# Residual gate early, four accumulator banks in the last jobs, another order of the last operands, and a shorter chain in the final norm

## The chip, the core and the metric

The kernel runs on one core of one Trainium2 chip. The time is the device time of one execution in microseconds (us). TensorE (PE in the profile) does the matrix products, VectorE (DVE), ScalarE (ACT) and GpSimd (POOL) the elementwise work, and SyncE (SP) issues nearly all transfers; a few go out on ACT's queue. Each engine and each queue takes its instructions strictly in the order in which the program gives them, and an instruction that waits for a semaphore holds up all behind it on that engine.

## The reference, cut to what matters

All is float32: a sequence of 2048 positions and a model width of 1024.

```python
mod = silu(c) @ w_mod + b_mod                       # (1, 3 * 1024)
shift, scale, gate = split(mod, 3)
h = rms_norm(x, g_norm) * (1 + scale) + shift
x_rnn, z_rnn, q, k, v, z_attn, g_r, g_a = split(h @ w_in, 8)      # each (2048, 1024)
y_rnn = (rg_lru(conv(x_rnn)) * silu(z_rnn)) @ w_out_rnn
y_attn = (dilated_attention(q, k, v) * silu(z_attn)) @ w_out_attn
merged = sigmoid(g_r + b_r) * y_rnn + sigmoid(g_a + b_a) * y_attn
x = x + gate * (merged @ w_o)
out = x * rsqrt(mean(x * x, -1) + 1e-6) * g_final
```

## The kernel before, in words

Every float32 product is three matmuls. Each operand is split into `hi`, its rounding to the short type fp32r, and `lo`, the rest; `mm3` (line 150) adds hi*hi, hi*lo and lo*hi. Line 158 (`hi_act`) is the rounding on ACT, line 164 (`lo_pool`) the subtraction on POOL, line 167 (`lo_dve`) the same on DVE. A split is therefore an ACT instruction followed by one on POOL or DVE, each on 128x512 numbers. The large products (`h @ w_in` and `merged @ w_o`) use a scheme of seven products of half-size blocks with sums of blocks as operands, in the manner of Strassen.

The order of all instructions is written by hand. Work beside the products is hung into them at a numbered place: a *slot* of the values, a *step* of the last jobs, a number of products done in the projections and the output. What is hung at a place is emitted ahead of the matmuls of that place, on whatever engine and queue it belongs to.

The stages that matter here, in order:

- **The second values** (about 727 to 828 us of the profiled execution): 8 runs of 4 slots; a slot is 24 matmuls with 256 columns. DVE, ACT and POOL at the same time build `hx` (the normed input), sums of its blocks in `t` and their splits into `T`, the operands of the next projections (lines 575 to 590, 738, 158, 167). `residual_gate` computes `gate` in these slots: `load` (line 1267) fetches a 128x512 piece `gw` of w_mod, `add` (lines 1272, 1274) multiplies it with a column of silu(c) into an accumulator, `total` sums the accumulator over its partitions by one matmul with ones, `bias` (line 1281) adds b_mod and sends the row to `gateD`, from which line 1962 later reads it back, spread over 128 partitions (`gate_b`).
- **The second projections** begin with product X, whose operand is `T`, and whose weights are raw pieces `R` (line 253) split into `S`.
- **The last jobs** (1981.95 to 2082.05 us): jobs 6 and 7 of the products with w_out_rnn and w_out_attn, 16 tiles t = 48 to 63 of 128x512, alternately of one and of the other job after the first four. A tile takes 8 steps of one `mm3` each; its accumulator is one PSUM bank. Its `load_g` (line 1851) fetches the two arrays `fg` with which the tile is merged, `evict` (lines 1856, 1858) multiplies and adds them on DVE, and `store` (line 1863) writes the sum to `meT`. There are four `fg` buffers, two tiles' worth, so the load for tile t waits for the store of tile t-2. The operands `yh`, `yl` of job 7 live in four of the 14 tiles `F`; they come from `oT` (line 359) and are split in place. Beside all that run the w_o operands: raw pieces `or` in four buffers (lines 1968, 1971), number i from 0 to 27, four to each of the seven operands in the order B11, T2, T3, T1, B21, T4, B22; those of B pieces are multiplied with `gate_b` (line 1976) and all are split into `F`.
- **The output products** (from 2082.05 us): 8 rounds x of seven products with 12 matmuls each: X (B11), Z (T2), W (T3), V (T1), X again (B21), Y (T4), and V again (B22), which is put behind the first product of the next round. V is a bank of pool `pf` in even rounds and of `pj` in odd ones. Their left operands are sums of blocks of `meT` (raw `R`, sums `s`, splits `S`). Lines 2170 and 2175 add banks into `u`, line 2124 adds banks to the rows `xo` (V twice, after T1 and after B22, and the second product may start only behind the first reading), line 2157 adds `u` on POOL.
- **The final norm** of each of the 16 row tiles: ACT squares and sums two halves (line 2135; the last two row tiles, line 2098), DVE adds the halves (line 2138, or 2106), line 171 scales and adds eps, ACT takes the root, and `rstd_last` (lines 176 to 180) forms the reciprocal with one Newton step; line 2145 scales the row, line 2147 stores it. These small instructions have 128x1 numbers, and four of a tile's seven on DVE have two tensor operands.

## Time and profile before

| | us |
|---|---|
| median of 3 runs (lowest, highest) | 2271.62 (2269.47, 2272.5) |
| the profiled execution, its time | 2262.82 |
| its span | 2261.0 |
| PE busy | 2202.5 |
| DVE busy | 1494.9 |
| ACT busy | 1293.2 |
| POOL busy | 1199.7 |

The profile is of one execution, which was 8.8 us shorter than the median. Durations, starts and waits in what follows are all of that execution. In a row of the timeline the first number is the start in us, the second how long the group lasted from its first start to its last end, `x12` is the number of instructions put together, and the bracket tells how long the engine was idle before it and what ended that. `L1274` is line 1274 of the kernel. SPq is SP's queue of transfers.

### The profile page before, as it was taken

The numbers are of one execution on the slowest core, as the hardware profiler recorded it, in microseconds if no ns is written. First come the engines' busy times: TensorE is split into PE (matmuls) and PEld (weight loads), VectorE is DVE, ScalarE is ACT, GpSimd is POOL, SyncE is SP. The second block draws the span as 40 slices with busy tenths as digits, with TensorE's granted clock in tenths as the row PEclk, the third lists the DMA queues.
The fourth block names the chain that finished last, engine by engine and source line by source line (L and its number), as shares of the span: only waits on it lengthen the run. The fifth ranks groups of instructions, "written<-read, shape, count | busy, mean of one in ns | idle before, by whom it ended". The sixth has DMA issues, their size and how long they took to land. (4 is left out here: it accounts for less than half of the span.)

```text
span 2261.0 us, 34371 instructions
## 1 busy us (share of the span) xinstructions
PE 2202.5 (97%) x11358; PEld 1846.4 (82%) x11359; DVE 1494.9 (66%) x2487; ACT 1293.2 (57%) x2560; POOL 1199.7 (53%) x898
## 2 busy tenths in 40 slices
PE   9999999999999999999999999999999999989898
PEld 5998888888877988888888887889889898867776
DVE  5578788778566665555545364466677878654898
ACT  3547667678543436656667511567678878532333
POOL 2267677676567345445444312356565666333666
PEclk9999999999999999999999999999999999999999
DMA  8354665565897556786887889989988787788543
GB/s 282 89 170 172 197 216 179 192 225 186 249 284 228 166 183 219 241 257 223 246 252 242 266 304 303 298 268 281 283 274 269 230 267 241 244 279 254 163 149 131
DMA packets 455434, 520.20 MB, mean 230 GB/s; under 512 B 90360, under 2 KB 333268, under 8 KB 454232
## 3 DMA queue, kind: packets, MB, share of 16 engines
q1 hardware_dynamic: 427492, 434.95, 63.3%
q10 hardware_dynamic: 27572, 83.00, 9.7%
q8 instruction: 90, 1.47, 0.3%
q14 instruction: 88, 0.72, 0.1%
q0 software_dynamic: 192, 0.05, 0.0%
HBM read 340.67 MB, written 177.21 MB: 229 GB/s over the span
## 5 line engine op out<-in xcount | busy, mean ns | idle before, releaser
L164 POOL TENSOR_TENSOR S<-R,S 128x512 fp32r<-128x512 f32 x278 | 407.9, 1473 | 401.5 <-ACT S L158 355.0
L150 PE MATMUL X<-T,S 128*128 128x512 f32 x1344 | 333.7, 397 | 6.1 <-ACT S L158 3.8
L150 PE MATMUL V<-T,S 128*128 128x512 f32 x1344 | 331.2, 395 | 0.0
L150 PEld LDWEIGHTS X<-T,S 128*128 128x128 f32 x1344 | 254.1, 190 | 67.6 <-ACT S L158 4.5
L150 PE MATMUL pj<-yh,S 128*128 128x512 f32 x896 | 302.2, 395 | 5.1 <-DMA S<-wD 3.3
L150 PEld LDWEIGHTS V<-T,S 128*128 128x128 f32 x1344 | 252.3, 188 | 58.3
L158 ACT ACTIVATE S<-R 128x512 fp32r<-128x512 f32 x278 | 170.8, 622 | 137.7 <-DMA R<-in_w_in_dram 114.8
L164 POOL TENSOR_TENSOR S<-s,S 128x512 fp32r<-128x512 f32 x108 | 160.4, 1485 | 144.3 <-ACT S L158 114.2
L150 PEld LDWEIGHTS pj<-yh,S 128*128 128x128 f32 x896 | 169.1, 189 | 41.0 <-DVE fg L1858 2.9
L150 PE MATMUL pj<-yl,S 128*128 128x512 f32 x448 | 176.4, 394 | 2.3 <-DVE yl L167 1.4
L1543 ACT ACTIVATE pp<-pp,st 128x256 f32<-128x256 f32 (+3 forms) x256 | 133.3, 522 | 74.7 <-DVE st L1542 74.3
L150 PE MATMUL Z<-T,S 128*128 128x512 f32 x672 | 165.5, 395 | 0.0
L150 PE MATMUL Y<-T,S 128*128 128x512 f32 x672 | 165.5, 395 | 0.0
L150 PE MATMUL W<-T,S 128*128 128x512 f32 x672 | 165.4, 395 | 0.0
L150 PEld LDWEIGHTS Z<-T,S 128*128 128x128 f32 x672 | 126.5, 188 | 30.5 <-issue 0.9
L150 PEld LDWEIGHTS Y<-T,S 128*128 128x128 f32 x672 | 126.5, 188 | 29.3
L150 PEld LDWEIGHTS W<-T,S 128*128 128x128 f32 x672 | 126.4, 188 | 29.3
L167 DVE TENSOR_TENSOR ptl<-pT,pth 128x384 fp32r<-128x384 f32 (+1 forms) x160 | 97.7, 627 | 48.8 <-ACT pth L158 46.6
L960 DVE SCALAR_TENSOR_TENSOR xc<-xr,par,xc 128x512 f32<-128x512 f32 x96 | 97.0, 1011 | 49.7 <-ACT xc L954 47.4
L1542 DVE CUSTOM_DVE_ANT_0 pp<-sc,msk 128x256 f32<-128x256 f32 (+3 forms) x256 | 104.1, 448 | 37.2 <-PE sc L150 35.0
L158 ACT ACTIVATE S<-s 128x512 fp32r<-128x512 f32 x108 | 67.3, 623 | 102.3 <-DVE s L290 44.7
L164 POOL TENSOR_TENSOR kq<-kraw,kq 128x512 fp32r<-128x512 f32 (+1 forms) x64 | 101.2, 1592 | 42.0 <-ACT kq L158 32.4
(367 smaller groups left out, 4840.6 us busy)
## 6 DMA issues: line engine op xcount, KB each, us to landing
sD<-S ACTq DMA_DIRECT2D x118, 512.0 KB, 3.8
S<-sD SPq DMA_DIRECT2D x118, 512.0 KB, 4.6
S<-wD SPq DMA_DIRECT2D x100, 512.0 KB, 5.4
R<-in_w_in_dram SPq DMA_DIRECT2D x196, 256.0 KB, 4.4
wD<-s ACTq DMA_DIRECT2D x64, 256.0 KB, 3.8
T<-in_w_mod_dram SPq DMA_DIRECT2D x8, 1024.0 KB, 12.1
vN<-ev SPq DMA_DIRECT2D x64, 128.0 KB, 2.8
zaT<-ev SPq DMA_DIRECT2D x32, 256.0 KB, 3.2
```

The costliest lines, as they stand in the source:

```text
L150: nc.tensor.matmul(o, lhsT=l, rhs=r, start=st, stop=sp, **kw)
L158: nc.scalar.activation(o, i, AF.Copy)
L164: nc.gpsimd.tensor_tensor(o, i, h.bitcast(F32), ALU.subtract)
L167: nc.vector.tensor_tensor(o, i, h.bitcast(F32), ALU.subtract)
L960: nc.vector.scalar_tensor_tensor(xc, xr[:, i : i + CH], cw(i), xc, ALU.mult, ALU.add)
L1542: nc.vector.tensor_tensor_reduce(pdst, s_ps, mask, 1.0, 3e38, ALU.add, ALU.min, m_)
L1543: nc.scalar.activation(pdst, pdst, AF.Exp, bias=m_, scale=-1.0, accum_out=l_)
```

## The change

Four parts, which touch different stages.

1. `residual_gate`: the 16 pieces are loaded at slots 0 to 15 and not 2 to 25, and each is added two slots later. There are three buffers `gw` instead of two, and each half of the gate has its own accumulator (`s1`, `s2`). `total` of half 0 stands at slot 10 and of half 1 at slot 19 (before: slot 16, and in the first products of the next projections), `bias` two slots later. The row of b_mod takes a `gw` buffer.
2. The last jobs: every third and fourth tile accumulates in the banks Z and W of the output products, so that four banks take turns; `evict` is hung at step 3 of the next tile (before: 1), `store` at step 6 (before: 5). The operands of job 7 are all loaded within job 6 and split there at other steps. Of the last two tiles, that of job 7 comes first.
3. The last operands of w_o: T4 (pieces 20 to 23) is split at steps 121 to 125 of 128, beside the last tile, and no longer in the output products; B22 (pieces 24 to 27) is loaded at steps 124 to 126 and at the start of the output products, and gated and split piece by piece, alternately on POOL and DVE.
4. The final norm: the squares are scaled so that their sum is the mean; the sum of halves and eps is one tensor-scalar instruction whose scalar is a column; the two multiplications of the Newton step are one such instruction, and the last multiplication is another. So five small DVE instructions stand where there were seven, none with two tensor operands.

Nothing else moves on any engine.

The end of the second values on DVE, before (`hx`, `t` and `T` are parts of the projections' operands, `s` the gate's accumulator, `ca` silu(c)):

```order
L1274 SCALAR_TENSOR_TENSOR s_1199_6837<-gw_7685,ca_194,s_1199_6837 128x512
L575 TENSOR_TENSOR t_1324_7831<-hx_7162,hx_7158 128x512
L577 TENSOR_TENSOR hx_7158<-hx_7158,T_6617 128x512
L167 TENSOR_TENSOR T_7484<-t_1321_7795,T_7483 128x512
L579 TENSOR_TENSOR hx_7158<-hx_7158,T_6618 128x512
L1274 SCALAR_TENSOR_TENSOR s_1199_6837<-gw_7717,ca_194,s_1199_6837 128x512
L584 TENSOR_TENSOR hx_7162<-hx_7162,hx_7158 128x512
L587 TENSOR_TENSOR t_1328_7898<-T_6768,hx_7162 128x512
L167 TENSOR_TENSOR T_7478<-hx_7158,T_7477 128x512
L167 TENSOR_TENSOR T_7480<-hx_7162,T_7479 128x512
L590 TENSOR_TENSOR t_1328_7898<-t_1328_7898,T_6769 128x512
L167 TENSOR_TENSOR T_7484<-t_1328_7898,T_7483 128x512
```

and with the change:

```order
L575 TENSOR_TENSOR t_1328_7842<-hx_7173,hx_7169 128x512
L577 TENSOR_TENSOR hx_7169<-hx_7169,T_6617 128x512
L167 TENSOR_TENSOR T_7509<-t_1326_7809,T_7508 128x512
L579 TENSOR_TENSOR hx_7169<-hx_7169,T_6618 128x512
L584 TENSOR_TENSOR hx_7173<-hx_7173,hx_7169 128x512
L587 TENSOR_TENSOR t_1331_7906<-T_6768,hx_7173 128x512
L167 TENSOR_TENSOR T_7503<-hx_7169,T_7502 128x512
L167 TENSOR_TENSOR T_7505<-hx_7173,T_7504 128x512
L590 TENSOR_TENSOR t_1331_7906<-t_1331_7906,T_6769 128x512
L167 TENSOR_TENSOR T_7509<-t_1331_7906,T_7508 128x512
```

The four additions of line 1274 that stood in this stretch (two here shown, two right behind it) are gone from it.

The start of job 6 on SP's queue, before (`fg` the arrays of a tile's merge, `S` split weights, `R` raw operands of job 7, `meT` the merged result):

```order
L359 DMA R_3926_20687<-oT 128x512
L359 DMA R_3927_20692<-oT 128x512
L1863 DMA meT<-fg_20597 128x512
L359 DMA R_3938_20725<-oT 128x512
L353 DMA S_3939_20727<-wD 128x1024
L359 DMA R_3942_20738<-oT 128x512
L359 DMA R_3943_20745<-oT 128x512
L1962 DMA gate_b_20716<-gateD 128x1024
L1851 DMA fg_20750<-gaT 128x512
L1851 DMA fg_20752<-mrT 128x512
L359 DMA R_3946_20757<-oT 128x512
L1863 DMA meT<-fg_20668 128x512
```

and with the change:

```order
L353 DMA S_3927_20684<-wD 128x1024
L1864 DMA meT<-fg_20599 128x512
L359 DMA R_3938_20723<-oT 128x512
L353 DMA S_3939_20725<-wD 128x1024
L359 DMA R_3942_20734<-oT 128x512
L359 DMA R_3943_20739<-oT 128x512
L1962 DMA gate_b_20714<-gateD 128x1024
L1852 DMA fg_20744<-gaT 128x512
L1852 DMA fg_20746<-mrT 128x512
L359 DMA R_3946_20751<-oT 128x512
L359 DMA R_3947_20761<-oT 128x512
L1864 DMA meT<-fg_20670 128x512
```

The two loads `R` that stood ahead of the first store are gone from there (the load `S` ahead of them in the first list with the change stands just above the rows of before); between the two `fg` of the next tile and the second store there are two loads `R` and not one.

The first round of the output products on DVE, before (`or` the raw pieces 24 to 27, `F` their splits, `u` sums of banks; the sum `u<-Z` of line 2170 stands two rows above the first):

```order
L2032 TENSOR_TENSOR s_4084_21553<-s_4083_21552,R_4057_21421 128x512
L1976 TENSOR_TENSOR or_21507<-or_21507,gate_b_20716 128x512
L1976 TENSOR_TENSOR or_21509<-or_21509,gate_b_20716 128x512
L1976 TENSOR_TENSOR or_21511<-or_21511,gate_b_20716 128x512
L1976 TENSOR_TENSOR or_21513<-or_21513,gate_b_20716 128x512
L2175 TENSOR_TENSOR u_4086_21563<-W_21539,u_4081_21536 128x512
L2041 TENSOR_TENSOR R_4062_21445<-R_4057_21421,R_4062_21445 128x512
L167 TENSOR_TENSOR F_21587<-or_21507,F_21586 128x512
L167 TENSOR_TENSOR F_21587<-or_21509,F_21586 128x512
L167 TENSOR_TENSOR F_21587<-or_21511,F_21586 128x512
L167 TENSOR_TENSOR F_21587<-or_21513,F_21586 128x512
L2124 TENSOR_TENSOR xo_21478<-V_21567,xo_21478 128x512
```

and with the change:

```order
L1976 TENSOR_TENSOR or_21451<-or_21451,gate_b_20714 128x512
L1976 TENSOR_TENSOR or_21463<-or_21463,gate_b_20714 128x512
L1976 TENSOR_TENSOR or_21469<-or_21469,gate_b_20714 128x512
L1976 TENSOR_TENSOR or_21498<-or_21498,gate_b_20714 128x512
L2182 TENSOR_TENSOR u_4085_21546<-Z_21521,u_4079_21519 128x512
L2036 TENSOR_TENSOR s_4087_21562<-R_4067_21458,R_4072_21489 128x512
L2037 TENSOR_TENSOR s_4088_21563<-s_4087_21562,R_4059_21423 128x512
L167 TENSOR_TENSOR F_21540<-or_21463,F_21539 128x512
L2187 TENSOR_TENSOR u_4090_21573<-W_21549,u_4085_21546 128x512
L2046 TENSOR_TENSOR R_4067_21458<-R_4059_21423,R_4067_21458 128x512
L167 TENSOR_TENSOR F_21540<-or_21498,F_21539 128x512
L2140 TENSOR_TENSOR xo_21496<-V_21577,xo_21496 128x512
```

The four multiplications by `gate_b` now stand ahead of the sum `u<-Z` (line 2182 with the change), two of the four subtractions of line 167 have gone to POOL, the other two are spread out ahead of line 2124 (2140 with the change).

SP's queue at the same place, before:

```order
L2020 DMA R_4062_21445<-meT 128x4x128
L1863 DMA meT<-fg_21390 128x512
L1863 DMA meT<-fg_21435 128x512
L2020 DMA R_4065_21471<-meT 128x4x128
L2037 DMA xo_21476<-in_x_dram 128x1024
L2037 DMA xo_21478<-in_x_dram 128x1024
L1971 DMA or_21507<-in_w_o_dram 128x512
L1971 DMA or_21509<-in_w_o_dram 128x512
L1971 DMA or_21511<-in_w_o_dram 128x512
L1971 DMA or_21513<-in_w_o_dram 128x512
```

and with the change:

```order
L1971 DMA or_21451<-in_w_o_dram 128x512
L2025 DMA R_4067_21458<-meT 128x4x128
L1971 DMA or_21463<-in_w_o_dram 128x512
L1971 DMA or_21469<-in_w_o_dram 128x512
L1864 DMA meT<-fg_21392 128x512
L1864 DMA meT<-fg_21444 128x512
L2025 DMA R_4072_21489<-meT 128x4x128
L2042 DMA xo_21494<-in_x_dram 128x1024
L2042 DMA xo_21496<-in_x_dram 128x1024
L1971 DMA or_21498<-in_w_o_dram 128x512
```

Three of the four loads of `or` have moved ahead of the last two stores; the fourth is still behind them, and behind a load `R` and two loads `xo`.

The diff, cut to its core:

```diff
     def residual_gate(ep, plan):
-        acc, row = (T(wq, [P, KH, P], F32, name, bufs=1)[:].rearrange("p k m -> p (k m)") for name in ("s1", "s2"))
-        row = row[:1]
-        w = {}
+        acc = [T(wq, [P, KH, P], F32, name, bufs=1)[:].rearrange("p k m -> p (k m)") for name in ("s1", "s2")]
+        w, row = {}, {}
...
+        def piece():
+            return T(ep, [P, CH], F32, "gw", bufs=3)
...
-            w[q, k] = T(ep, [P, CH], F32, "gw", bufs=2)
+            w[q, k] = piece()
...
         def total(q):
+            row[q] = piece()
+            nc.sync.dma_start(row[q][:1, :], b_mod[0:1, 2 * D + q * CH : 2 * D + (q + 1) * CH])
             w["pt"] = T(pg, [P, CH], F32, "pg")
-            mm(w["pt"][:1, :], ones[:, 0:1], acc, True, True)
+            mm(w["pt"][:1, :], ones[:, 0:1], acc[q], True, True)
...
         for q in range(2):
             for k in range(KT):
-                i = 2 + 13 * q + (3 * k) // 2
+                i = KT * q + k
                 at_slot(i, lambda q=q, k=k: load(q, k))
-                at_slot(i + 3, lambda q=q, k=k: add(q, k))
-            at_slot(5 + 13 * q, lambda q=q: nc.sync.dma_start(row, b_mod[0:1, 2 * D + q * CH : 2 * D + (q + 1) * CH]))
-            if not q:
-                at_slot(16, lambda: total(0))
-                at_slot(17, lambda: bias(0))
-        later(1, lambda: total(1))
-        later(2, lambda: bias(1))
+                at_slot(i + 2, lambda q=q, k=k: add(q, k))
+            at_slot(10 + 9 * q, lambda q=q: total(q))
+            at_slot(12 + 9 * q, lambda q=q: bias(q))
...
-        tiles += [(LAST_HEAD + i, m) for m in range(2, KT) for i in range(2)]
+        tiles += [(LAST_HEAD + (i ^ (m == KT - 1)), m) for m in range(2, KT) for i in range(2)]
...
-            ps = T(pj, [P, CH], F32, "pj")
+            ps = T(pj, [P, CH], F32, "pj") if j < LAST_HEAD or t % 4 < 2 else FP["bank"](t % 4 - 2)
...
-                if k == 1 and t:
+                if k == (1 if j < LAST_HEAD else 3) and t:
                     evict(t - 1, last)
                 if k == 3:
                     load_g(t)
-                if k == (7 if j < LAST_HEAD else 5) and t:
+                if k == (7 if j < LAST_HEAD else 6) and t:
                     store(t - 1)
...
-                            if k in (5, 6):
-                                load_y(j + 2, k - 5)
...
-                    if i in (0, 1, 2, 3, 6, 7):
-                        load_y(j + 1, i + 2 if i < 4 else i)
-                    if i in (1, 2, 5, 6, 8, 9, 11, 12):
-                        split_y(LAST_HEAD + 1, (1, 2, 5, 6, 8, 9, 11, 12).index(i))
+                    if i in (0, 1, 2, 3, 5, 6, 7, 8):
+                        load_y(LAST_HEAD + 1, i - (i > 3))
+                    if i in (4, 5, 6, 7, 10, 11, 12, 13):
+                        split_y(LAST_HEAD + 1, i - (4 if i < 8 else 6))
...
+        FP["bank"] = lambda i: T(pf, [P, CH], F32, "ZW"[i])
...
-            (lo_dve if i % 2 or i >= 20 else lo_pool)(F[name][1][:, k, :], raw_o.pop(i)[:], F[name][0][:, k, :])
+            (lo_dve if i % 2 else lo_pool)(F[name][1][:, k, :], raw_o.pop(i)[:], F[name][0][:, k, :])
...
-            if i < 20:
+            if i >= 20:
+                at_step(101 + i, lambda i=i: hi_o(i))
+                at_step(102 + i, lambda i=i: lo_o(i))
+                if i > 20:
+                    at_step(103 + i, lambda i=i: load_o(i + 3))
+            else:
...
-        late_parts = [(0, hi_o, i) for i in range(20, 24)] + [(0, lo_o, i) for i in range(20, 24)]
-        late_parts += [(1, load_o, i) for i in range(24, 28)] + [(3, gate_o, i) for i in range(24, 28)]
-        late_parts += [(4, fn, i) for fn in (hi_o, lo_o) for i in range(24, 28)]
+        late_parts = [(0, load_o, 27)]
+        for i in range(24, 28):
+            late_parts += [(d + (i - 24) // 2, fn, i) for d, fn in ((1, gate_o), (2, hi_o), (3, lo_o))]
...
+        def first_root(ss):
+            nc.vector.tensor_scalar(ss[:, 0], ss[:, 0], ss[:, 3], EPS, ALU.add, ALU.add)
+            nc.scalar.activation(ss[:, 1], ss[:, 0], AF.Sqrt)
+
+        def last_root(ss):
+            v, y, t = (ss[:, i] for i in range(3))
+            nc.vector.reciprocal(y, y)
+            nc.vector.tensor_scalar(t, y, y, v, ALU.mult, ALU.mult)
+            nc.vector.tensor_scalar(t, t, -0.5, 1.5, ALU.mult, ALU.add)
+            nc.vector.tensor_scalar(y, y, t, None, ALU.mult)
...
-            nc.scalar.activation(jk[:], xo[:, cols], AF.Square, accum_out=ss[:, 3 if whole else 0])
+            nc.scalar.activation(jk[:], xo[:, cols], AF.Square, scale=D ** -0.5, accum_out=ss[:, 3 if whole else 0])
...
-                tt(ss[:, 0], ss[:, 0], ss[:, 3], ALU.add)
-                rstd(ss)
+                first_root(ss)
+                last_root(ss)
```

20 lines of the change are left out of this document (9 added, 11 removed).

## The prediction

> **What bounds the kernel now.** PE is busy for 2202.5 of 2261.0 us, so only the stretches where it is not can be won; I looked for them with a list of 20-us windows, then read the waits of PE there, and the timeline at each. These are the windows that matter (length; busy us of PE, weight loads, DVE, ACT, POOL; granted clock, share of DMA, GB/s):
>
> ```profile
> 800.00:820.00 20.00, 18.24 (x151) 17.84 (x149) 19.14 (x20) 8.93 (x16) 10.36 (x8) 1.00 0.35 101
> 820.00:840.00 20.00, 16.29 (x76) 12.90 (x77) 6.17 (x8) 5.06 (x9) 5.44 (x4) 0.83 0.71 224
> 1980.00:2000.00 20.00, 14.91 (x59) 11.41 (x57) 7.53 (x9) 5.12 (x9) 6.84 (x6) 0.91 0.88 273
> 2100.00:2120.00 20.00, 12.87 (x45) 9.94 (x45) 17.18 (x23) 8.76 (x19) 13.65 (x10) 0.74 0.34 107
> 2120.00:2140.00 20.00, 20.00 (x88) 16.35 (x87) 19.44 (x28) 7.37 (x18) 14.09 (x12) 1.00 0.52 157
> ```
>
> PE loses 1.8 and 3.7 us at the end of the values (with DVE at 19.14 of 20 ahead of it), 5.1 at the start of job 6 and 7.1 in the first output round, the clock falling below 1 in the last three of these windows; in the output rounds PE is full but DVE is too (19.44 of 20). What PE waited for from 1940 us to the end (total, times, longest):
>
> ```profile
> PE V L150 <- DVE xo L2124: 8.8, 3, 7.1
> PE pj L150 <- DVE fg L1856: 5.6, 6, 2.6
> PE pj L150 <- DMA S<-wD: 2.5, 1, 2.5
> PE pj L150 <- DVE xo L2124: 1.7, 2, 1.2
> ```
>
> That is 18.6 us, and slow-clock time on top; at the end of the values there is one more wait, of 3.39 (below). Every part of the change touches one of these waits, and nothing else in the order moves, so I cost them one by one.
>
> **Term 1, the gate in the values.** The chain that ends the stage:
>
> ```profile
> 822.71 0.68 DVE L590 TENSOR_TENSOR t<-t,T 128x512 f32<-128x512 f32 x1
> 823.42 0.63 ACT L158 ACTIVATE T<-t 128x512 fp32r<-128x512 f32 x1 [3.78 <-DVE t L590]
> 826.62 0.44 SPq L253 DMA_DIRECT2D R<-in_w_in_dram  x1
> 830.06 0.63 ACT L158 ACTIVATE S<-R 128x512 fp32r<-128x512 f32 x1 [5.04 <-DMA R<-in_w_in_dram]
> 830.75 1.03 PE L150 MATMUL X<-T,S 128*128 128x512 f32 x2 [3.39 <-ACT S L158]
> L1272 DVE TENSOR_SCALAR s<-gw,ca x2: 477/478/479, 744.4 to 788.8; 128x512 f32<-128x512 f32 x2
> L1274 DVE SCALAR_TENSOR_TENSOR s<-gw,ca,s x14: 739/746/1771, 748.8 to 825.5; 128x512 f32<-128x512 f32 x14
> ```
>
> Late DVE holds ACT's split of `t`; ACT's copies of the values come behind it, their stores hold SP's queue, and the weights `R` that X needs stand in that queue behind them. So X starts as late as DVE is. DVE works without a gap from about 776 us to the end of L590. In that stretch stand seven additions, the first multiplication of half 1 and one `bias`; with the change, which adds the last piece at slot 17 and puts `total` and `bias` of half 1 at slots 19 and 21, there are four additions and one `bias`. Three additions at the median 0.746 and one multiplication at 0.478 go: X comes 2.7 us earlier. Against it: the gate crowds into the first slots, where `total` of half 0 needs the eighth addition; I reckon 0.2 us of waiting there. Part of X runs at half clock, and I leave that as it is. SP's queue will stand before the `gw` loads up to some 6 us, waiting for a buffer; the raw weights behind these are used eight slots after their load, and a slot is 24 matmuls, so that covers it. The gain is bounded by the wait of 3.39 and, if X's clock stays full, one X of twelve matmuls (2.94 in a later row), 6.3 in all; the loss, if the crowd delays the first `hx`, by one addition in its slow form, 1.77. **-2.5**.
>
> **Term 2, the last jobs.**
>
> ```profile
> 1988.00 4.93 SPq L359 DMA_DIRECT2D R<-oT  x2
> 1990.03 0.47 PE L150 MATMUL pj<-yh,S 128*128 128x512 f32 x1 [2.48 <-DMA S<-wD]
> 1993.45 0.42 SPq L1851 DMA_DIRECT2D fg<-gaT  x1
> 1999.96 6.08 PE L150 MATMUL pj<-F,S 128*128 128x512 f32 x24 [2.61 <-DVE fg L1856]
> 2081.51 0.56 SPq L1851 DMA_DIRECT2D fg<-gaT  x1
> 2084.84 2.95 PE L150 MATMUL Z<-F,S 128*128 128x512 f32 x12
> 2086.34 0.69 DVE L1856 TENSOR_TENSOR fg<-pj,fg 128x512 f32<-128x512 f32 x1 [3.17 <-DMA fg<-gaT]
> 2087.63 2.94 PE L150 MATMUL W<-F,S 128*128 128x512 f32 x12
> ...
> SPq L1851 <- DMA meT<-fg: 27.7, 10, 3.8
> ...
> meT<-fg SPq DMA_DIRECT2D x16, 256.0 KB, 5.0
> R<-oT SPq DMA_DIRECT2D x6, 256.0 KB, 6.9
> ```
>
> The loads of `fg` set the pace, not the banks: from the load at 1993.45 (tile 48) to that at 2081.51 (tile 63) are 15 tiles in 88.06 us, 5.87 each, where 24 matmuls need 5.58 (from Z's start to W's, 12 of them in 2.79). Each load waits for the store two tiles back to land (27.7 us of SP's waits). Four banks don't shorten that loop; they only let PE run ahead of it by two tiles more. But PE pays at the end: product W takes the bank of tile 63 and waits for its `evict`. So the gain is how much sooner tile 63 is merged. The loop starts sooner, since the load for tile 48 stood behind two `R` of job 7 for which SP waited (4.93 with their issue, row at 1988.00); with the change two loads `R` fewer stand ahead of that `fg` pair. Of the 4.93 about 1 is issue and another 1 goes to the store that now stands ahead; I take 2.9 us, so `evict` of tile 63 ends at 2085.7 and not at 2088.6, and W, now freed by its first instruction, can start at about 2083.4, 4.2 us before 2087.63. From the PE side the excess of tiles 48 to 63 over 5.58 us each is 11.4 us, so PE could be there in time.
>
> The cost is in job 7's operands: its pieces 4 to 7 are loaded behind the splits of pieces 0 to 3 and needed four steps into tile 50 (1999.96 less its wait of 2.61, and half of 5.58 on: 2000.1). The first leave about when the row at 1988.00 does, some 0.6 later; ready is 1988.6 plus two landings L, so PE waits S = 2L - 11.5: none at the 5.0 us of a store, 2.3 at the 6.9 of `R<-oT`. I take none, for these loads leave before the merge traffic fills the queue, and keep 2.3 for the range. **-4.2 at W**, of which the next term says what reaches the end.
>
> **Term 3, the first output round.**
>
> ```profile
> 2090.68 2.32 SPq L1971 DMA_DIRECT2D or<-in_w_o_dram  x4
> 2097.09 3.02 DVE L1976 TENSOR_TENSOR or<-or,gate_b 128x512 f32<-128x512 f32 x4 [2.05 <-DMA or<-in_w_o_dram]
> 2098.66 2.96 PE L150 MATMUL X<-F,S 128*128 128x512 f32 x12
> 2101.23 6.76 DVE L167 TENSOR_TENSOR F<-or,F 128x512 fp32r<-128x512 f32 x4
> 2108.74 5.46 PE L150 MATMUL V<-F,S 128*128 128x512 f32 x12 [7.13 <-DVE xo L2124]
> 2114.00 1.27 PE L150 MATMUL Z<-F,S 128*128 128x512 f32 x4
> ```
>
> B22's raw pieces are issued at 2090.68, land 6.4 us later, are gated, and then four subtractions take 6.76 us on DVE (1.7 each: POOL is at work on tensors of its own), and the addition that frees V stands behind them. V costs 7.13 of waiting, and 5.26 us to the next product where 2.79 is the rule, 2.5 of half clock: 9.6 in all. With the change pieces 24 to 26 come earlier, beside the last tile, but piece 27 stands behind two stores, a load `R` and two `xo` on SP. The second store waits for `evict` of tile 63 (2085.7), so it leaves at about 2088.1 and lands at 2094.5. Its gating stands on DVE **ahead** of `u<-Z`, which then comes at about 2095 and not at 2091.60, and on POOL the addition of `u` to `xo` stands ahead of the split that product X of round 1 needs. So X of round 1 starts at about 2098.3, as before, though PE is there at 2094.5 (the next wait: about 3.8 us). POOL has two of the four subtractions; the second comes behind two `xo` and one `S`, 2104 to 2106 by POOL's row-to-row pace of 1.3 to 1.7. V then runs till some 2107.5 with part of it at half clock. Z of round 1 starts at 2107.5 and not at 2114.0: **-6.5 for terms 2 and 3 together**. Bounds: all 9.6 of term 3 and 4.2 of term 2 gone is -13.8; only the slack between the two orders of the four subtractions, 2 of 1.7 us less on DVE, is -2.
>
> **Term 4, the norm's small instructions.**
>
> ```profile
> L177 DVE TENSOR_TENSOR ss<-ss x16: 159/814/1283, 2115.0 to 2255.6; 128x1 f32<-128x1 f32 x16
> L178 DVE TENSOR_TENSOR ss<-ss x16: 159/1210/1226, 2116.4 to 2255.8; 128x1 f32<-128x1 f32 x16
> L179 DVE TENSOR_SCALAR ss<-ss x16: 153/154/156, 2116.5 to 2256.0; 128x1 f32<-128x1 f32 x16
> L2138 DVE TENSOR_TENSOR ss<-ss x14: 144/1165/1246, 2111.7 to 2241.5; 128x1 f32<-128x1 f32 x14
> ...
> 2235.14 2.95 PE L150 MATMUL Z<-F,S 128*128 128x512 f32 x12
> ```
>
> On one number per partition the form with two tensors takes up to 1.28 us, the tensor-scalar form never over 0.156: the first waits for POOL and the second does not. The three slow ones, 3.19 us a row tile by their medians, become two pointer forms. No row shows a pointer form of 128x1; between 0.154 (its nearest kin) and 1.21 I take 0.2, since both shapes and forms are those of L179 but for where the scalar lies. That frees 2.8 us of DVE in each 10 us, and the waits of the rounds go: from Z of round 1 (2114.00) to Z of round 7 (2235.14) are 121.1 us, where six rounds of seven products at 2.79 need 117.2. Excess 3.9; PE's waits for line 2124 but for the one of 7.1 sum to 3.4. **-3.3** (0 to -3.9).
>
> The Trainium skill says the opposite may happen: in SBUF — State Buffer, section "Who interferes with whom", `tensor_scalar` may enter a mode with both ports that shuts GpSimd out or waits for it. By that rule the merged ones would wait as L178 does, and this term would be near 0. L179 in the rows above, with 154 in the middle of 16, does not bear that out.
>
> **Term 5, the tail.**
>
> ```profile
> 2248.95 2.88 PE L150 MATMUL pj<-F,S 128*128 128x512 f32 x12
> 2253.09 0.68 DVE L2092 TENSOR_TENSOR xo<-pj,xo 128x512 f32<-128x512 f32 x1
> ```
>
> PE ends at 2251.83 (2248.95 and 2.88); the last addition waits until the first row tile's chain is through, 2253.09. That chain loses two instructions and its slow forms, some 0.8 us by the slow forms in the rows of term 4, and the last row tile's own loses two instructions at 0.15: **-1.1** (-0.2 to -1.5).
>
> **Sum.** -2.5 - 6.5 - 3.3 - 1.1 = -13.4. The profiled execution took 2262.82, so 2249.4 on its scale. It was 8.8 us under the median of 2271.62, to which the change is measured: **2258**.
>
> **The rivals.**
> - *Piece 27 does not hold anything.* If it lands in time, or the queue is shorter, all 13.8 of terms 2 and 3 come through: -20.7, 2251. For it: the medians of landings above are 5.0 and 6.9 us, and the stores ahead could leave at once. Against: the order itself, with gating ahead of `u<-Z`.
> - *The merged norm instructions wait like the old ones.* Then term 4 falls away and term 5 shrinks to 0.2: -9.2, 2262. For it, beside the page named above: no pointer form of this size is in the trace.
> - *Job 7's operands come late.* At a landing of 6.9, S is 2.3 and the half clock that followed a gap of 2.48 (granted clock 0.91 in that window) adds 1.9, part of which is taken up by waits behind it: -10.5, 2261. The same mechanism gives the other sign: the pieces 4 to 7 wait in one queue with eight loads and the merge traffic, and if a landing takes 14.8 us, S is 18.1 and eats the 13.4 and 4.5 more: 2276 or above. The longest median in the stage is 6.9, so this needs twice the traffic's delay.
> - *The waits only move.* DVE or POOL takes back in the rounds what PE wins at V: within 4.5 us of the median, 2271. For it: DVE is at 19.4 of 20 until term 4 frees it, and POOL gets four tensors more.
>
> The Trainium skill has a rule on the half clock, in TensorE: Matmul & The Clock Gate, Part 1: after an idle window of about 3.4 us the clock falls to half. The 2.48 us before 1990.03 were followed by slow matmuls, so a shorter gap does it in this trace; by the page's rule a gap of 3.8 before X of round 1 would be sure to cost, by the row it may, and my sum has it in V's end.
>
> **How the numbers follow.** Chances: the forecast 0.43, all of term 3 gone 0.14, merged forms that wait 0.12, operands a little late 0.12, waits that only move 0.09, operands so late that it is slower 0.10. 0.2% is 4.5 us, about what three runs here can tell from nothing. Faster by more: the first four, 0.81; same 0.09; slower 0.10. The range reaches from 2247, all of terms 2 and 3 gone and terms 1 and 4 at their bounds in part, to 2268, where two of the smaller terms fail at once; outside lie the last two cases. For the forecast alone I expect 2254 to 2262.
>
> **What would show it.** Term 1: X's first matmul near 828 instead of 830.75. Term 2: no waits `pj <- fg`, but a wait of product W. Term 3: the V wait of 7.1 gone, a new wait of X in round 1 on a split by POOL, Z of round 1 near 2104 (2107.5 less term 1). Term 4: the merged rows near 0.2 us, DVE in 2120 to 2140 near 16 of 20. I am wrong if the pointer rows have a median over 0.8, if tile 50 waits over 5 us, or if X of round 1 does not wait.

## The result

The change makes the kernel faster: 2259.91 us (median of 5 runs, 2258.11 to 2266.53) against 2269.47 us (5 runs on the same chip, 2267.33 to 2272.5). The ratio is 0.9959, with a 95% interval of 0.9941 to 0.9977, or 9.3 us. Predicted were 2258 and a gain of 13.4.

The profiled execution after took 2258.11 us, its span 2256.0; that of before had 2261.0. The two spans differ by 5.0 us only, because the changed one lost 4.6 us ahead of the first place that the change touches (the second values begin at 731.95 us and not at 727.34). So the times are read by stretches between the same PE instructions in both programs: the *values* from the first product of the second values to product Z of the projections behind them, the *jobs* from the first product behind the attention to the first output product X, the *first round* from there to Z of round 1, the *rounds* from there to Z of round 7, and the *tail*.

| us | values | jobs | first round | rounds | tail |
|---|---|---|---|---|---|
| before | 109.27 | 107.66 | 31.95 | 121.14 | 25.86 |
| after | 107.73 | 103.58 | 33.39 | 116.21 | 24.77 |
| difference | -1.54 | -4.08 | +1.44 | -4.93 | -1.09 |

The differences sum to -10.2, near the 9.3 of the runs. The page after, its first group, and the windows that answer to those of before:

```profile
PE 2201.3 (98%) x11359; PEld 1845.6 (82%) x11359; DVE 1456.7 (65%) x2451; ACT 1294.0 (57%) x2560; POOL 1215.1 (54%) x902
```

```profile
800.00:820.00 20.00, 20.00 (x170) 20.00 (x169) 19.83 (x19) 8.33 (x15) 13.27 (x9) 1.00 0.33 100
820.00:840.00 20.00, 14.98 (x95) 13.21 (x94) 7.30 (x7) 6.06 (x11) 6.08 (x4) 0.83 0.53 165
1980.00:2000.00 20.00, 16.07 (x64) 12.83 (x63) 7.51 (x9) 6.32 (x10) 6.13 (x6) 0.91 0.86 275
...
2100.00:2120.00 20.00, 15.33 (x53) 11.29 (x52) 16.59 (x21) 9.02 (x19) 17.18 (x12) 0.83 0.43 139
2120.00:2140.00 20.00, 20.00 (x89) 16.28 (x88) 16.45 (x26) 7.44 (x18) 17.42 (x12) 1.00 0.55 170
```

In the rounds VectorE has fallen from 19.44 to 16.45 of 20 us. In the first round PE still loses 4.7 of 20 us. PE's waits from 1940 us to the end, after (total, times, longest):

```profile
PE X L150 <- POOL S L164: 4.2, 1, 4.2
PE pj L150 <- DMA S<-wD: 3.9, 1, 3.9
PE Z L150 <- DVE fg L1857: 1.5, 1, 1.5
PE W L150 <- DVE fg L1857: 1.2, 1, 1.2
PE V L150 <- POOL F L164: 0.5, 1, 0.5
PE Z L150 <- ACT F L158: 0.4, 1, 0.4
PE Z L150 <- DVE F L167: 0.2, 1, 0.2
PE Z L150 <- POOL F L164: 0.2, 1, 0.2
```

All waits of before are gone but that for the weights; in their place stand X's wait for a split on GpSimd, and those of banks Z and W for the merge of the last tiles. The last three rows are tile 50, which now accumulates in bank Z and waits for operands of job 7. The last jobs and the first round on the timeline:

```profile
1987.68 2.45 SPq L359 DMA_DIRECT2D R<-oT  x1
1993.73 0.32 SPq L1852 DMA_DIRECT2D fg<-gaT  x1
1995.14 0.47 PE L150 MATMUL pj<-yh,S 128*128 128x512 f32 x1 [3.93 <-DMA S<-wD]
...
2083.82 0.63 SPq L1852 DMA_DIRECT2D fg<-gaT  x1
2090.30 3.04 PE L150 MATMUL W<-F,S 128*128 128x512 f32 x12 [1.21 <-DVE fg L1857]
2095.14 0.42 SPq L1971 DMA_DIRECT2D or<-in_w_o_dram  x1
2101.44 0.69 DVE L1976 TENSOR_TENSOR or<-or,gate_b 128x512 f32<-128x512 f32 x1 [4.49 <-DMA or<-in_w_o_dram]
2102.05 0.68 DVE L2182 TENSOR_TENSOR u<-Z,u 128x512 f32<-128x512 f32 x1
2102.82 1.64 POOL L2169 TENSOR_TENSOR xo<-xo,u 128x512 f32<-128x512 f32 x1 [7.01 <-DVE u L2182]
2104.42 1.71 POOL L164 TENSOR_TENSOR S<-R,S 128x512 fp32r<-128x512 f32 x1
2106.18 4.63 PE L150 MATMUL X<-F,S 128*128 128x512 f32 x10 [4.16 <-POOL S L164]
2115.02 1.32 PE L150 MATMUL Z<-F,S 128*128 128x512 f32 x5
```

Here is the chain that the prediction named: piece 27 leaves at 2095.14, lands 6.3 us later, its gating holds `u<-Z`, that holds GpSimd, and X of round 1 waits 4.16 us. And here is what it did not foresee. The load of `gaT` for tile 48 leaves 15.68 us behind the first product of the jobs (1978.05), where it left at 19.06 before: 3.4 us sooner. But that for tile 63 leaves at 105.77, where it left at 107.12: only 1.35 sooner. The head start is lost in the loop's first turn. This stands on SP's queue between the loads for tiles 48 and 49, before and then after:

```profile
1994.45 0.38 SPq L359 DMA_DIRECT2D R<-oT  x1
1994.88 0.64 SPq L1863 DMA_DIRECT2D meT<-fg  x1
1995.61 1.08 SPq L359 DMA_DIRECT2D R<-oT  x2
...
1999.05 0.33 SPq L1851 DMA_DIRECT2D fg<-gaT  x1
```

```profile
1995.74 2.91 SPq L359 DMA_DIRECT2D R<-oT  x2
1998.70 0.42 SPq L1864 DMA_DIRECT2D meT<-fg  x1
1999.68 4.25 SPq L359 DMA_DIRECT2D R<-oT  x3
...
2004.99 0.43 SPq L1852 DMA_DIRECT2D fg<-gaT  x1
```

Five loads `R` of job 7's operands stand there and not three, and SP waits ahead of them for splits (from 1987 to 2007 us 2.9 us for those of `F` on GpSimd and 1.8 for those on VectorE). The load for tile 49 waits for nothing but its place: it leaves directly behind the last `R` and two other loads. It does so 26.95 us behind the first product and not 24.66, which is 2.3 later than before. From there to tile 63 a tile takes 5.63 us, where it took 5.89. The loop itself has not become slower; only its mean from tile 48 on has (6.01 and not 5.87).

The norm's small instructions after:

```profile
L2095 DVE TENSOR_SCALAR ss<-ss x16: 200/202/214, 2114.2 to 2249.9; 128x1 f32<-128x1 f32 x16
...
L2101 DVE TENSOR_SCALAR ss<-ss x16: 272/273/275, 2116.4 to 2250.6; 128x1 f32<-128x1 f32 x16
L2102 DVE TENSOR_SCALAR ss<-ss x16: 153/154/155, 2116.7 to 2250.9; 128x1 f32<-128x1 f32 x16
L2103 DVE TENSOR_SCALAR ss<-ss x16: 214/215/217, 2116.9 to 2251.1; 128x1 f32<-128x1 f32 x16
```

No pointer form waits once in 48. One scalar column costs about 0.05 to 0.06 us more than an immediate, two about 0.12.

### The profile page after: what moved, and what is told of

Same layout as the page of the kernel before. It is cut to its first block, busy times and chain, and to the rows that moved or that the text cites. A ratio compares the mean times of both kernels' runs of the same rounds, so it can differ in the third digit from the quotient of the medians.

```text
span 2256.0 us, 34354 instructions
## 1 busy us (share of the span) xinstructions
PE 2201.3 (98%) x11359; PEld 1845.6 (82%) x11359; DVE 1456.7 (65%) x2451; ACT 1294.0 (57%) x2560; POOL 1215.1 (54%) x902
## 4 chain that ended last, share of the span: by engine, by line
PE 48%; DMA 10%; DVE 3%; issue 3%; ACT 2%; POOL 2%; SPq 1%; ACTq 0%; POOLq 0%; DVEq 0%
PE X L150 9%; PE pj L150 9%; PE V L150 7%; PE W L150 4%; PE Z L150 4%; PE Y L150 4%; PE sc L150 4%; PE o L150 4%; DMA fg<-mrT 1%; DMA meT<-fg 1%; PE pg L150 1%; PE pT L1628 1%; DMA wo<-in_w_o_dram 1%; PE pT L1641 1%; DMA R<-in_w_in_dram 1%
## 5 line engine op out<-in xcount | busy, mean ns | idle before, releaser
L150 PE MATMUL pj<-yh,S 128*128 128x512 f32 x848 | 287.8, 397 | 4.6 <-DMA S<-wD 3.9
L164 POOL TENSOR_TENSOR S<-s,S 128x512 fp32r<-128x512 f32 x108 | 165.9, 1537 | 128.7 <-ACT S L158 97.0
L150 PEld LDWEIGHTS pj<-yh,S 128*128 128x128 f32 x848 | 160.9, 190 | 37.9 <-DVE fg L1859 4.3
L150 PE MATMUL pj<-yl,S 128*128 128x512 f32 x424 | 167.5, 395 | 2.1 <-DVE yl L167 1.2
```

The source lines that it names most:

```text
L150: nc.tensor.matmul(o, lhsT=l, rhs=r, start=st, stop=sp, **kw)
L164: nc.gpsimd.tensor_tensor(o, i, h.bitcast(F32), ALU.subtract)
```

## The experiments

The theory was: the norm's two-tensor instructions made VectorE the limit of the rounds; the loads of the merge arrays, not the banks, pace the last jobs; and piece 27 held the first round. The main rival was that the parts only move waits to one another. Each kernel was timed against the kernel before on the same chip, and the experiments went to three chips, so ratios are compared and not times; the stretches are of its profiled execution.

| | values | jobs | first round | rounds | tail | ratio to before (95%) |
|---|---|---|---|---|---|---|
| change | 107.73 | 103.58 | 33.39 | 116.21 | 24.77 | 0.9959 (0.9941 to 0.9977) |
| without gate | 111.23 | 103.65 | 34.18 | 116.22 | 24.71 | 0.9975 (0.9965 to 0.9985) |
| two banks | 107.91 | 107.09 | 30.29 | 116.27 | 24.72 | 0.9959 (0.9944 to 0.9975) |
| without norm | 106.87 | 103.59 | 34.76 | 123.90 | 25.94 | 1.0004 (0.9991 to 1.0017) |
| norm alone | 109.69 | 107.34 | 31.84 | 116.52 | 24.74 | 0.9966 (0.9950 to 0.9982) |
| without operands | 107.71 | 102.82 | 39.19 | 116.35 | 24.73 | 0.9961 (0.9946 to 0.9975) |
| piece 27 early | 107.88 | 103.22 | 32.12 | 116.27 | 24.71 | 0.9942 (0.9927 to 0.9958) |
| piece 27, weights first | 107.67 | 102.75 | 34.22 | 116.27 | 24.78 | 0.9941 (0.9924 to 0.9959) |
| third pair | 106.73 | 103.32 | 24.11 | 116.23 | 24.70 | 0.9900 (0.9880 to 0.9920) |
| third pair on before | 109.14 | 106.45 | 29.56 | 121.67 | 25.91 | 0.9986 (0.9975 to 0.9997) |
| third pair, two banks | 107.56 | 106.14 | 23.64 | 116.21 | 24.76 | 0.9925 (0.9906 to 0.9944) |
| third pair, weights first | 107.97 | 103.61 | 23.68 | 116.21 | 24.70 | 0.9911 (0.9890 to 0.9931) |
| all three | 107.80 | 103.31 | 22.23 | 116.20 | 24.74 | 0.9901 (0.9881 to 0.9920) |

### The norm, taken back and alone

```diff
-                first_root(ss)
-                last_root(ss)
+                tt(ss[:, 0], ss[:, 0], ss[:, 3], ALU.add)
+                rstd(ss)
```

and the same at the other row tiles. 

> The changed kernel, but with the final norm's seven small VectorE instructions of before. Theory: the two-tensor forms wait for GpSimd; the six output rounds go from 116.2 us back to 120 to 121, VectorE to over 18 of 20 us there, the tail from 24.8 to 25.9; the whole is 5 to 6 us longer. Rival: what sped up the rounds is that the operands of the second round start better after the changed first round, and the rounds stay within 1 us of 116.2.

The rounds take 123.90 us, more than the 120 to 121 expected, and the window that answers to those above shows PE short and VectorE full again:

```profile
2120.00:2140.00 20.00, 18.68 (x81) 14.96 (x80) 19.32 (x28) 7.37 (x18) 14.09 (x11) 1.00 0.51 157
```

The rounds are longer than in the kernel before (121.14), which has the same instructions there. There the first two of the six rounds took 19.6 and 19.7 us and the others 20.2 to 20.8; here every one takes 20.3 to 21.0. That fits VectorE having done a part of the first rounds' work in the 7 us in which PE waited for V, but no run takes this apart. So what the other parts win ahead of the rounds, VectorE takes back in them: the whole is at 1.0004. By the stretches the norm's part is worth 9.4 us here, and not the 5 to 6 expected. The rival on the operands of round 2 falls.

The reverse, the kernel before with the norm's new instructions (the diff of the change, its part of the norm): 

> The kernel before with the norm's new instructions alone. Theory: in the output rounds VectorE was the limit, so this alone brings the rounds from 121.1 us to 116.3 and the tail from 25.9 to 24.7, about 6 us, and leaves the first output round at 31.9; the ratio to the kernel before is about 0.9974. Rival: the other three parts make up the rest of the change's 9 us only together with the norm, since what they won was taken back by VectorE in the rounds; then this alone gives 6 and they 3 more. If this alone gives 9 or more, the other parts are worth nothing.

The rounds come to 116.52 and the tail to 24.74 as expected, 5.7 us; the ratio says 7.7. Alone it gives 0.9966, with the rest 0.9959. The intervals overlap: beside the norm, the three other parts are not shown to win anything in the time, though by the stretches they win some 4.5 us more.

### The gate, taken back

```diff
-                i = KT * q + k
+                i = 2 + 13 * q + (3 * k) // 2
```

with its accumulator and buffers. 

> The changed kernel, but the residual gate stands in the values as before (pieces at slots 2 to 25, one accumulator, two buffers). Theory: the gate's late additions on VectorE cost 1.5 to 2.7 us at the end of the values, so the stretch from the first matmul of the second values to product Z of the projections behind them takes about 109.3 us again (it was 109.27 before and 107.73 with the change), and the whole time grows by 1.5 to 2.5. Rival: the two profiles differ there by chance (the changed one began that stretch 4.6 us later and PE waited 4.89 for its weights and not 3.39), and the stretch stays within 0.5 of 107.7.

The stretch takes 111.23 us. Over all profiles of this study it took 109.14 to 111.23 with the old gate (4 kernels, mean 109.8) and 106.73 to 107.97 with the new (10 kernels, mean 107.6), so 2.2 us by the means, with no overlap. The ratio moves from 0.9959 to 0.9975, and the two intervals overlap. The theory holds, the size by the stretches alone. Of the 2.2 us, 1.3 are the start of X (102.2 us behind the first product by the means, and not 103.5); most of the rest is that `total` of half 1 no longer stands on PE between X and Z.

### The banks, taken back

```diff
-            ps = T(pj, [P, CH], F32, "pj") if j < LAST_HEAD or t % 4 < 2 else FP["bank"](t % 4 - 2)
+            ps = T(pj, [P, CH], F32, "pj")
```

with the merge at step 1 and the store at step 5. 

> The changed kernel, but all tiles of the last jobs accumulate in the two banks of before, with the merge at step 1 and the store at step 5. Theory: the loads of the merge arrays pace the tiles, so the banks only let PE run ahead: the tiles take 3 to 5 us longer (103.6 to about 107.5 from the last attention product to the first output product), the first output round gets about as much shorter, since products Z and W no longer wait for a merge, and the sum of both (136.97) stays within 1.5. Rival: the four banks carry the gain of the stage, and the sum goes to 140 or more.

The jobs take 3.5 us longer and the first round 3.1 less; the sum is 137.38 against 136.97, and the ratio is the same. As the theory has it, four banks let PE run ahead and wait at Z and W.

### Piece 27 and the operands

```diff
-        late_parts = [(0, load_o, 27)]
+        at_step(126, lambda: load_o(27))
+        late_parts = []
```

> The changed kernel, but the last piece of w_o (27) is loaded right behind piece 26, ahead of the last two stores, two loads of x rows and one raw load. Theory: what cost the first output round its gain is this piece, whose gating stood on VectorE ahead of the sum from bank Z (2102.05) and, through it, ahead of the split for product X of round 1, which PE awaited for 4.16 us: that wait falls to 1 or less, the stretch from the first output product to Z of round 1 goes from 33.4 to 28 to 30 us, and the whole is 3 to 5 us shorter. Rival: GpSimd's queue or the late merge of the last two tiles sets it anyway; then the wait only moves to product V and the stretch stays over 32.

X's wait of 4.16 is gone, but these take its place:

```profile
PE W L150 <- DVE fg L1857: 2.6, 1, 2.6
PE Z L150 <- DVE fg L1857: 2.1, 1, 2.1
PE V L150 <- DVE xo L2141: 1.5, 1, 1.5
PE V L150 <- POOL F L164: 1.1, 1, 1.1
```

The jobs and the first round together are 1.6 us shorter, not 3 to 5, and the ratio of 0.9942 is not clear of 0.9959. The first round takes 32.12, where the rival put it (over 32). Both theory and rival had a part: the chain was there, and behind it the late merge of the last tiles. That the merge is late was the better lead.

Taking the whole of part 3 back (T4's splits in the output products and on VectorE, B22's loads behind the last stores): 

> The changed kernel, but the operands T4 and B22 are loaded, gated and split where they were before (T4 at the start of the output products, all of their lo parts on VectorE, the four loads of B22 after the last stores). Theory: the wait of product V for VectorE (7.1 before) comes back at about 5 to 7 us, the wait of product X of round 1 for a GpSimd split (4.2) falls to under 1; the stretch from the last attention product to Z of round 1 is 1 to 3 us longer than with the change (136.97). Rival: the two waits are worth the same and this part of the change gives nothing: within 1 of 137.

The wait of V is back at 8.0 us and the first round takes 39.19. The jobs and it sum to 142.0, 5.0 more than with the change and more than the 1 to 3 expected, so this part earns its place in the profile. The ratio, 0.9961, is that of the change, and the two intervals together are just wide enough to hide 5 us. How much of it is of that one execution stays open.

### The loop of the merge arrays

The tiles' loads had four buffers, two pairs. There is no room for a third in that pool, but job 6 leaves one tile of each operand ring idle:

```diff
+            third = j >= LAST_HEAD and t % 3 == 2
+            if third and not spare:
+                spare.extend(T(fl, [P, CH], F32R, tag, bufs=NY)[:].bitcast(F32) for tag in ("yh", "yl"))
...
-                g = T(fl, [P, CH], F32, "fg", bufs=4)
+                g = spare[i] if third else T(fl, [P, CH], F32, "fg", bufs=4)[:]
```

> The changed kernel with a third pair of merge arrays in the last jobs (two otherwise idle tiles of the operand ring), so that a load no longer waits for the store two tiles back but three. Theory: the loads wait for buffers, and with a third pair the merges keep up with PE: the waits of products Z and W for a merge (1.5 and 1.2) go to under 0.5, and the stretch from the first output product to Z of round 1 falls by 1 to 3 us. Rival: the transfers themselves are full (0.85 to 0.95 of the DMA engines' time), so the loads come no sooner and nothing changes by more than 0.5.

The loads of `gaT` of tiles 48 and 63 in this kernel, and Z of round 1:

```profile
1987.83 0.32 SPq L1855 DMA_DIRECT2D fg<-gaT  x1
...
2068.76 0.64 SPq L1855 DMA_DIRECT2D fg<-gaT  x1
...
2099.97 2.95 PE L150 MATMUL Z<-F,S 128*128 128x512 f32 x12
```

That is 80.93 us for 15 tiles, 5.40 each and no more 6.01. The first turn still takes 11.4 us, as in the change; from tile 49 on a tile takes 4.97 and no more 5.63. The waits of Z and W are gone, the store of the last tile leaves early, piece 27 with it, and X no longer waits. The first round falls by 9.3 us, more than the 1 to 3 expected; all that stood behind the loop's end came forward with it. The time is 2247.32 us, 0.9900. The transfers were not full, though DMA was busy for 0.85 and more: with the third pair its share in the windows from 2000 to 2080 us is 0.96 to 1.00, where it was 0.85 to 0.95. The rival falls.

The third pair on the kernel before: 

> The kernel before with the third pair of merge arrays alone (two banks, job 7's operands, last operands, norm and gate as before). Theory: the buffers of the merge arrays are what paced the last jobs in both kernels, so here the waits of the tiles for a merge (5.6 us in all) go to under 1 and the last tile is merged sooner; but the four loads of B22 stand behind the last stores and the four VectorE splits ahead of V's reading stay, and VectorE limits the rounds, so the stretch to Z of round 1 shortens by 4 to 7 us (139.6 to about 134) and the whole by 2 to 5. Rival: the third pair is worth the same 9.6 us in that stretch as on the changed kernel.

Jobs and first round sum to 136.0 against 139.6, 3.6 us and a little less than the 4 to 7 expected, and the rounds stay at 121.67; the time falls by 0.14%, 3 us. The waits of the tiles for a merge fall from 5.6 to 3.1 only, not to under 1. So the same edit is worth 9.6 us in that stretch on the changed kernel and 3.6 on the old: there V still waits 4.7 us for VectorE.

With two banks: 

> The changed kernel with the third pair of merge arrays and the two banks of before (merge at step 1, store at step 5). Theory: once the loads keep up, two banks are enough, as a merge takes 1.4 of the 5.6 us of a tile: the stretch from the last attention product to Z of round 1 stays within 1.5 of the 127.4 of four banks. Rival: without the banks PE waits again at the tiles, and the stretch goes over 130.

The sum is 129.78, 2.35 more than with four banks (127.43), between what theory and rival gave. PE then waits three times for a merge, 0.4 to 0.7 us each, and once 0.85 for an operand of job 7. Once the loads keep up, the four banks do earn something in these two profiles, about 2 us; the intervals of the two ratios overlap.

### The weights of tile 49

```diff
-                    if i in (0, 1, 2, 3, 5, 6, 7, 8):
-                        load_y(LAST_HEAD + 1, i - (i > 3))
+                    if i in (1, 2, 3, 5, 6, 7, 8):
+                        for q in (0, 1) if i == 1 else (i - (i > 3),):
+                            load_y(LAST_HEAD + 1, q)
```

On piece 27's kernel, and on the third pair's: 

> The changed kernel with piece 27 loaded behind piece 26, and in job 6 the weights for the second half of tile 49 loaded ahead of job 7's operands, which now stand one step later. Theory: PE's wait for these weights (3.7 to 3.9) falls to 1 to 2, since they stood 2.4 us behind a load that waited for a buffer; but the merge arrays pace the tiles, so what PE wins is given back at the banks Z and W, and the whole gains 0 to 1 us against piece 27 alone. Rival: PE's start in job 6 sets the stage; then 2 us remain at the end.

> The changed kernel with the third pair of merge arrays, and the weights for tile 49 loaded ahead of job 7's operands. Theory: the merges no longer pace the tiles, so what PE wins at tile 49 (its wait of 3.5 falls to 1 to 2.5, and it took 2.4 us of standing behind a load) now reaches the end: 1 to 2 us shorter than 127.4 in the stretch. Rival: job 7's operands then come late by as much, a wait takes its place at tile 50, and the stretch does not change.

PE's wait for the weights stayed at 3.1 and 4.0, and did not fall to 1 to 2.5. In the second kernel this is the load that was put first:

```profile
1989.06 2.94 SPq L353 DMA_DIRECT2D S<-wD  x1
```

Its issue itself took 2.94 us, where the median of this line is 0.376. In the changed kernel the load `R` at that place took 2.45 (row at 1987.68). The delay does not belong to the load that stands there, and it does not always come: on piece 27's kernel with the weights first no issue at that place took over 0.9 us, and PE waited 3.1 all the same. So theory and rival on tile 49 both fall: its wait hardly got shorter, and no wait over 1.1 us came at tile 50. On piece 27's kernel the time is the same (0.9941 and 0.9942), as the first theory had it for the whole. There Z of round 0 now waits 4.8 us for a split on ACT; it stands behind a sum on VectorE, which stood behind a merge that had waited 4.56 us for its `gaT`. That is one more sign of the late merges.

All three together: 

> The changed kernel with the third pair of merge arrays, the weights for tile 49 ahead of job 7's operands, and piece 27 loaded behind piece 26. Theory: with the third pair the stores come early enough for piece 27, so its place is worth less than 1 us here; the time is that of the third pair with the weights ahead, about 2245. Rival: the gain of piece 27's place (33.4 to 32.1 in the first stretch of the output) adds in full, another 1.5 to 3 us.

The first round falls to 22.23, another 1.9, as the rival had it (1.5 to 3); in the runs it is not told from the third pair alone: 2245.07 us, 0.9901, against 2247.32, 0.9900. Either beats the kernel before by 1.0% and the change by 0.6%.

## Why the prediction was right

- **The time.** 2258 was predicted and 2259.91 measured; of the 13.4 us there came 9.3 (10.2 by the stretches). That the two times lie closer than the two gains is luck: the kernel before came at 2269.47 us this time and not at 2271.62.
- **Term 1, the gate: right in mechanism, too large.** -2.5 was put down; the pair of profiles shows -1.54 and all of them 2.2. X did not start near 828 but at 834.47, since the whole stage began 4.6 later in that execution; a start in absolute time was the wrong thing to name. Within the stage X starts 0.9 us sooner in this pair and 1.3 by the means, not 2.5. From VectorE's last long wait to the end of L590 it took 45.8 us and not 48.5, 2.7 less, as reckoned (partly by luck, as two of the four additions left ran in the slow form, and VectorE waited once less). But `total` of half 0 costs more than the 0.2 of waiting put down for it. This is its row after, and the end of that long wait before and after:

```profile
774.86 0.69 DVE L167 TENSOR_TENSOR b12l<-hx,b12h 128x512 fp32r<-128x512 f32 x1 [3.69 <-ACT hx L539]
```

```profile
765.46 1.02 PE L150 MATMUL pg<-s,ones 128*1 128x512 f32 x2 [0.21 <-DVE s L1276]
...
780.89 0.69 DVE L167 TENSOR_TENSOR b12l<-hx,b12h 128x512 fp32r<-128x512 f32 x1 [2.32 <-ACT hx L539]
```

With its wait, `total` now stands on PE ahead of the transposes from which the last `hx` are made, so VectorE's last long wait ends 48.94 us behind the start of the stage and not 47.52, 1.4 later. And the 1.8 us that PE waited for splits of `S` at product V in the slots before are gone, but for the most part they come back at X, where PE waits 4.89 us and not 3.39.

- **Term 2, the last jobs: the mis-sized step.** It said that a loop which starts 2.9 us sooner ends 2.9 us sooner, and W with it 4.2. The loop did start 3.4 sooner. But the loads `R` that the change puts between its first two turns ate this: the first turn took 11.3 us and not 5.6. In the eleven profiles with this order of loads it took 11.2 to 11.4, in the three with the old one 5.1 to 5.7. The prediction had counted these loads as a risk for PE at tile 50, and not for the load of `fg` behind them in the queue. The later turns took 5.63 us and not 5.89 (5.6 to 5.9 in all kernels without a third pair, with either order of loads), so the last `evict` began at 111.41 behind the first product of the jobs and not at 111.95, 0.5 sooner and not 2.9. The other slip is in the sum: it lets W start as the merge's first instruction starts, but W can only start as that ends, 0.7 us later. W came at 112.25 and not at 113.24, 1.0 sooner. That the buffers bound the later turns is shown by the third pair; no run moves the loads `R`, so what their place costs the whole is not shown.
- **Job 7's operands** were not late for PE: tile 50 waited 0.87 us for them in three pieces, and the rival of the other sign did not come. What their loads cost the loop is in term 2.
- **Term 3: right in mechanism and size.** W to Z of round 1 was put at 24.1 and took 24.72 (before: 26.37); the wait of X at 3.8, measured 4.16; behind piece 27 and GpSimd, as said. Terms 2 and 3 together were -6.5 and came to -2.6; of the gap of 3.9 us, 3.2 stand at W and are of term 2.
- **Term 4: right, and larger.** -3.3 was put down and -4.9 came. The pointer forms cost 0.20 to 0.27, near the 0.2 taken, and the bound of -3.9 was too tight since a round at full pace takes 116.2 / 6 = 19.4 us and not 19.5. The rule of the Trainium skill that `tensor_scalar` may contend with GpSimd (SBUF — State Buffer, "Who interferes with whom") does not show at this shape: none of the 48 pointer rows took over 0.28 us. With four numbers per partition it may: in the kernel before, L179 took 0.17 us three times and 1.22 once (747.47), and that one ended within 0.1 us of a subtraction on GpSimd. The Trainium skill's rule, in the same section, that two SBUF inputs contend agrees with the old rows, 0.14 to 0.16 us at the lowest and up to 1.28. But no run takes GpSimd away, so that it is GpSimd they wait for is not shown apart.
- **Term 5: right**, -1.09 for -1.1.
- **Three small sums** are off and bear on nothing: 2107.5 less term 1 is 2105 and not 2104, 18.1 less 13.4 is 4.7 and not 4.5, and from 1981.95 to 2082.05 the excess of the tiles over 5.58 us each is 10.8 and not 11.4.
- **The rival that the waits only move** was given 0.09. It is what happens without the norm's part (1.0004); with it, VectorE has room, and the gain stays.

The clock: X of round 1 after its gap of 4.16 us ran ten matmuls in 4.63, half speed. In the kernel with piece 27 early, gaps of 2.14 and 2.61 us, 3 us apart, had the same effect on W:

```profile
2092.44 4.58 PE L150 MATMUL W<-F,S 128*128 128x512 f32 x12 [2.61 <-DVE fg L1857]
```

The idle window of about 3.4 us in the Trainium skill (TensorE: Matmul & The Clock Gate, Part 1) doesn't tell when single gaps below it cost; here 2.48 did and one of 2.61 didn't. The granted clock of the traces gives a lead. Its stretches of half speed last 3.41 us or a multiple, and what counts may be how busy PE was in the 3.41 us just ahead. Before, PE was busy for 1.50 us from 1988.12 to 1991.53, and the clock from there to 1994.94 was 0.50. The gap of 2.61 was split over two such windows, with 2.41 and 1.80 us busy, and no slow one followed. In the kernel with piece 27 early PE was busy for 0.80 us from 2089.75 to 2093.16, and the clock behind that was 0.50. No run was made on this.

## What to carry to other kernels

Where a loop of loads, merges and stores through few buffers paces a stage, more banks are given back in it, and of a head start only that counts which the second turn keeps: measure its period at the issues of one load, the first turn apart from the later ones, look at what else the change puts into that queue, and look for one more buffer first. Where an engine is full in the last stage, whatever is won ahead of it is lost there until that engine is relieved: relieve it first, and here the relief was a form of instruction with one tensor input. Say in advance the length of a stretch between two of PE's instructions, not a time from the start, since the same code began a stage up to 6.8 us apart from execution to execution (725.58 to 732.39).

## What had not been expected

In ten of the fourteen profiles the issue of one transfer on SP took 2.1 to 2.9 us at one place of job 6, whether a load `R` or `S` stood there, against a median of 0.33 to 0.43 for these lines; in the other four no issue there took over 1.4. It is not a wait on a semaphore in the trace; what it waits for stays open. And a third pair of buffers took 9.3 us from a stretch in which PE's waits for the merges themselves were but 2.7 us: the rest was the chain of stores and loads behind them, and matmuls at half clock.
